# One decoder layer on one core: first heads copied within SBUF, statistics of mixer C at other hooks, output weights in rotating buffers, residual loads on the sync queue

## The chip, the core and the metric

The kernel runs on one core of one Trainium2 chip. The metric is the device time of one execution in microseconds (us); the core's five engines are TensorE (PE, with its weight loads PEld), VectorE (DVE), ScalarE (ACT), GpSimd (POOL) and SyncE (SP), and 16 DMA engines move data between DRAM and the on-chip memory SBUF. PE writes its products to PSUM, from where DVE or ACT take them. SP, ACT and POOL each have a queue of their own on which they issue DMAs, in their program's order; an instruction that waits holds up all that stand behind it on its engine.

## The reference, cut to what matters

One layer of a hybrid decoder on x (1024 positions, width 1024), all in float32:

```python
h = rmsnorm(x, norm_mix_g)
a_h, a_b, a_c, q, k, v, c_val, c_gate = split(h @ w_in)     # 256 x3, 512 x3, 256 x2
y_a = a_b * causal_dwconv(a_c * a_h, conv_a_w)              # 3 taps
y_b = dilated_mixture(q, k, v, rel_bias)                    # 8 heads of 64, three dilations
u   = causal_dwconv(c_val * sigmoid(c_gate), conv_c_w) + conv_c_b   # 31 taps
y_c = silu(layernorm(u, ln_c_g, ln_c_b))
y   = concat(rmsnorm(y_a, g_a), rmsnorm(y_b, g_b), rmsnorm(y_c, g_c))
x   = x + y @ w_out
up  = causal_dwconv(rmsnorm(x, norm_ffn_g) @ w_up, conv_f_w)
x   = x + (silu(gate) * val) @ w_down
return rmsnorm(x, final_g)
```

What matters here: y_c needs three statistics over its 256 channels one after another (the mean, the variance, then the mean square for the last norm), each of which needs the one before. q and k of a head are needed whole before its first score. And w_out is applied to y_a and y_c (128-row blocks 0, 1, 6, 7) and to y_b (blocks 2 to 5) in two separate stages.

## The kernel before, in words

Every float32 matrix product is made of three products of rounded parts: an operand is split into a high part (ACT casts it, line 71) and a low part (the difference, line 72, on POOL or DVE), and `mm3` (lines 90 to 92) adds hi x hi, hi x lo and lo x hi. A product is 128 x 128 by 128 x 512 columns.

**Input projections.** `proj` (line 252) computes one 128-column block of h @ w_in: eight steps (one for each block of 128 rows), six products in each. `load_w` brings its weights into the pair of rotating buffers `w_raw`, `w_hi`, `w_lo` (two of each), so the weights of block n+2 can be split only when the products of block n are done. After each step `proj` runs the functions that were hooked to that step. From line 421 the blocks are, with the count of their first step: `ah` of half 0 (step 8), `ac` (16), `ab` (24), `ah` of half 1 (32), `ac` (40), `ab` (48), then q and k of heads 0 and 1 (`proj_qk(0)` at 56, `proj_qk(4)` at 64), of heads 2 and 3 (`proj_qk(1)` at 72, `proj_qk(5)` at 80). The four other pairs follow during the attention (`more_qk`, line 607).

**Statistics of mixer C.** DVE does the 31 taps of the long convolution (line 298) while these blocks run, and adds the two halves (`ln_a`, line 432). `stat_hook` (line 268) hooks two things to later steps: `first`, in which PE sums over the channels (line 116, eight one-column results) and DVE and ACT finish the statistic, and then `col_to_rows`, in which PE turns the column into rows (line 137), DVE copies them, and SP writes them to DRAM and reads them back as a row for all partitions (lines 142 and 146). What follows is handed on: `ln_center` (line 447) subtracts the mean, `ln_scale` (line 453) scales and applies silu, and the last row goes to `norm` (line 435). The steps are in `HK` (line 466): `HK[0]`, `HK[1]` for the mean, counted from step 40; `HK[2]`, `HK[3]` counted from the step at which `ln_center` ran; `HK[4]`, `HK[5]` counted from the step of `ln_scale`. With 6, 8, 8, 10, 9, 11 the three sums come at steps 46, 56, 67 and the rows at 48, 58, 69. `HK[6]`, `HK[7]` (steps 61 and 65) are those of mixer A. PE's order is fixed by the program, so a statistic that isn't ready at its step stops PE.

**Heads.** `proj_qk` writes the high and low part of q and k to DRAM (`qk`, lines 397 and 398, on SP). `load_head` (line 488) brings a head's rows back as `sa` (high part of q in both halves of the partitions), `sb` (low part of q) and `sm` (high and low part of k): six transfers of 256 KB on POOL's queue, then the bias strip `g` on SP and v on POOL. It is called for heads 0 and 1 at line 516, after the last `proj_qk` and after the pools for the attention are opened.

**Attention.** PE works through chunks of scores, transposes and p x v products (lines 527, 528, 550, 581). Between them `slot` (line 713) takes steps from `fill`, that is `more_qk` and then `out_ac` (line 658): the products of y_a and y_c with w_out, in two halves of 512 output columns (`dh`), eight blocks of 128 positions (`t`) each, four products (three matmuls each) to a block. `out_ac` opens its pools in the room of the normalised input (`close(c_x)`), splits the four y tiles (two of them, of y_c, come from DRAM through `w_raw`), then loads w_out with `load_half` into `w_raw` and splits it into `wac` (dh 0) and into `w_hi`, `w_lo` (dh 1). The residual x (`xp2`, eight tiles of 512 KB) is loaded on ACT's queue, held behind the last cast of those weights (line 689), and added at line 700. `pair_den` (line 592) sends the denominators of a pair of heads to DRAM and back on SP (lines 142 and 597) and `finish_pair` (line 601) multiplies by them on DVE.

**What sets the order.** PE's order is the program's. For the other engines a planner picks at build time, from its own estimate of times, which ready instruction an engine takes next, the earlier in the program first; `issue_after` pins an instruction behind another one on its engine. So a transfer whose buffer is free is issued well ahead of its place in the program. A tile in a pool opened in the room of another pool waits only for the tiles whose room it takes.

Of the kernel before, what the change touches and what calls it, by code (L numbers as in the profile page):

```python
# [9 lines left out]
F32 = mybir.dt.float32  # L10
# [4 lines left out]
P = 128  # L15
# [21 lines left out]
def body(tc, x_t, x_n, grow, par, cst, rel, oneh, nlnc, wc, w_cols, wv, w_out, w_up, w_down, out):  # L37
# [14 lines left out]
    def close(*cms):  # L52
        for cm in cms:
            cm.__exit__(None, None, None)
# [11 lines left out]
    def f(ap):  # L66
        return ap.bitcast(F32)

    def split(src, hi, lo, lo_eng, g=None):
        if g is None:  # L70
            cp = A.copy(hi, src)  # L71
            lo_eng.tensor_tensor(out=lo, in0=src, in1=f(hi), op=ALU.subtract)  # L72
        else:
            cp = A.activation(out=hi, in_=src, func=AF.Copy, scale=g)
            V.scalar_tensor_tensor(out=lo, in0=src, scalar=g, in1=f(hi), op0=ALU.mult, op1=ALU.subtract)
        return cp
# [26 lines left out]
    def table(func, after=None):  # L103

        with tc.issue_after(mark[after].ins) if after else ExitStack():
            c = const.tile([P, 8], F32, name="st_c", tag="st_c", bufs=4)
            A.activation(out=c[:, :1], in_=ones, func=func)
# [273 lines left out]

    qk = [dr.tile([2, P, S], F32, name=f"qk{i}") for i in range(8)]

    def proj_qk(i, pos, tmp=None):
        ps = proj(pos, "qk")
        t = tmp[0] if tmp else evt("qt")
        if i < 4:
            V.scalar_tensor_tensor(out=t[:, :S], in0=ps, scalar=-0.125, in1=r1b, op0=ALU.mult, op1=ALU.mult)
        else:
            V.tensor_tensor(out=t[:, :S], in0=ps, in1=r1b, op=ALU.mult)  # L390
        if tmp:
            hi, lo = tmp[1:]
        else:
            hi = ev.tile([P, S], F32R, name="q_hi", tag="fr", bufs=6)
            lo = ev.tile([P, S], F32R, name="q_lo", tag="fr", bufs=6)
        split(t[:, :S], hi, lo, G if tmp else V)
        nc.sync.dma_start(out=qk[i][0], in_=f(hi))
        nc.sync.dma_start(out=qk[i][1], in_=f(lo))

# [61 lines left out]
    def do_norm():  # L461
        while todo:
            norm(*todo.pop())

    todo = []
    HK = (6, 8, 8, 10, 9, 11, 5, 9)
    stat_hook(lna, 1.0 / 256, None, HK[0], HK[1], ln_center)
    a_conv(1, t1)
    a_out(1, t1)
# [4 lines left out]
    do_norm()  # L474
    proj_qk(1, 9)
    do_norm()
    table(AF.Exp, "sqrt")
    proj_qk(5, 10, (yb[2], yb[3].bitcast(F32R), yb[2].bitcast(F32R)))
    close(c_ev, c_mm)
# [4 lines left out]
    for n, bufs in (("T", 2), ("S", 1), ("F", 1), ("L", 1), ("V", 2)):  # L484
        pss[n] = pool("ps" + n, space=PS, bufs=bufs)
    psS, psL, psT, psV, psF = (pss[n][1] for n in "SLTVF")

    def load_head(h):
        j, s = h // 2, (h % 2) * 64
        sa = a0.tile([P, S], F32R, name="sa", tag="sa", bufs=2)  # L490
        sb = a0.tile([P, S], F32R, name="sb", tag="sb", bufs=2)
        sm = a0.tile([P, S], F32R, name="sm", tag="sm", bufs=2)
        g = a0.tile([P, S], F32, name="g", tag="g", bufs=2)
        vv = a0.tile([P, TT, P], F32R, name="vv", tag="vv", bufs=2)
        for dst, src in ((sa, (qk[j][0], qk[j][0])), (sb, (qk[j][1], qk[j][1])), (sm, (qk[4 + j][0], qk[4 + j][1]))):
            for e in range(2):
                G.dma_start(out=dst[e * 64:(e + 1) * 64, :], in_=src[e][s:s + 64, :])
        fr = fs[h:h + 1, 1:1 + S]
        fr = bass.AP(tensor=fr.tensor, offset=fr.offset, ap=[[1, P], [1, S]])
        nc.sync.dma_start(out=g, in_=fr)  # L500
        G.dma_start(out=vv, in_=vd[:, :, h * P:(h + 1) * P].rearrange("t p c -> p t c"))
        return sa, sb, sm, g, vv

    NPT = 3
    pth = [a1.tile([P, 4 * P], F32R, name=f"pth{i}") for i in range(NPT)]
# [7 lines left out]
    den = [a1.tile([P, 16], F32, name=f"den{j}") for j in range(4)]  # L513
    mn = a1.tile([P, 64], F32, name="mn")
    SEG = {0: [256], 1: [256], 2: [384], 3: [512], 4: [512, 256], 5: [512, 256], 6: [512, 384], 7: [512, 512]}
    heads = {0: load_head(0), 1: load_head(1)}

    def score(h, qi):
        sa, sb, sm, g, _ = heads[h]
# [118 lines left out]
    def load_half(rows, dh, hi, lo):  # L638

        raw = wp.tile([P, 1024], F32, name="w_raw", tag="w_raw", bufs=2)  # L640
        nc.sync.dma_start(out=raw.rearrange("p (b c) -> p b c", b=2),
                          in_=w_out[rows * P:(rows + 2) * P, dh * 512:dh * 512 + 512]
                          .rearrange("(b p) c -> p b c", b=2))
        mark["w"] = split(raw, hi, lo, G)

    def load_row(k, hi, lo):
        raw = wp.tile([P, 1024], F32, name="w_raw", tag="w_raw", bufs=2)
# [9 lines left out]

    def out_ac():

        close(c_x)  # L660
        held["xp"], px = pool("xp", "right")
        held["wac"], pw = pool("wac", "right")
        held["yac"], pa = pool("yac", "right")
        for i in AC:
            yh[i] = pa.tile([P, S], F32R, name=f"yh{i}")
            yl[i] = pa.tile([P, S], F32R, name=f"yl{i}")
        wac = [(pw.tile([P, 1024], F32R, name=f"wac_hi{q}"), pw.tile([P, 1024], F32R, name=f"wac_lo{q}"))
               for q in range(2)]
        held["x4"] = px.tile([P, 4, S], F32, name="x4")
        xp2.extend(held["x4"][:, t, :] for t in range(4))  # L670
        for t in range(4, 8):
            xp2.append(px.tile([P, S], F32, name=f"xp{t}"))
        for i in AC:
            t = yb[2 + i] if i < 2 else wp.tile([P, 1024], F32, name="w_raw", tag="w_raw", bufs=2)
            if i >= 2:
                nc.sync.dma_start(out=t, in_=yd[i % 4])
            with tc.issue_after(mark["t"].ins), tc.issue_after(mark["v"].ins):
                split(t, yh[i], yl[i], V)
            yield 0
        for dh in range(2):  # L680
            w2 = wac if dh == 0 else [wp_pair() for _ in range(2)]
            for q, r in enumerate((0, 6)):
                load_half(r, dh, *w2[q])
            if dh:
                for q in range(2):
                    load_row(2 + q, *wac[q])
            for t in range(8):
                if dh == 0:
                    with tc.issue_after(mark["w"].ins):
                        for q in ((0, 1) if t == 0 else (t + 1,) if t < 7 else ()):  # L690
                            nc.scalar.dma_start(out=xp2[q], in_=x_n[q * P:(q + 1) * P, :])
                ps = psF.tile([P, 512], F32, name="f_ps", tag="f_ps")
                ts = slice(t * P, (t + 1) * P)
                for n, k in enumerate(AC):
                    cs = slice(n % 2 * 512, n % 2 * 512 + 512)
                    mm3(ps, yh[k][:, ts], yl[k][:, ts], w2[n // 2][0][:, cs], w2[n // 2][1][:, cs], n == 0, n == 3)
                    if n < 3:
                        yield 1
                x2 = xp2[t][:, dh * 512:dh * 512 + 512]
                V.tensor_tensor(out=x2, in0=ps, in1=x2, op=ALU.add)  # L700
                yield 2
        for q in range(2):
            load_row(4 + q, *wp_pair())

    def both():
        yield from more_qk()
# [459 lines left out]
```

## Time and profile before

| what | value |
|---|---|
| median of 3 runs | 1182.11 us (1181.99 to 1182.67) |
| the profiled execution | 1181.71 us |
| its span, first to last instruction | 1179.9 us |
| PE busy | 1138.5 us, 96% |
| DVE, ACT, POOL busy | 757.4, 503.7, 521.3 us |
| mean granted TensorE clock | 0.984 of full speed |
| DMA | 162.80 MB, mean 138 GB/s |

How to read it: a busy PE is not PE at its peak, since matmuls overlap; at full speed a 512-column matmul starts about every 0.23 us though it is shown with 0.39. [...] All times within the execution are counted from the first instruction. "DMA share" is the busy share of the 16 DMA engines, and can read above 1. In the list of waits, a line says who waited for whom, the sum, how often, and the longest.

### The profile page before, as it was taken

What the parts mean: (1) busy time and instruction counts of PE and PEld (TensorE: products, weight loads), DVE (VectorE), ACT (ScalarE), POOL (GpSimd) and SP (SyncE); (2) the same over time, 40 slices, a digit from 0 to 9 for tenths busy, and PEclk for the clock granted to TensorE, in tenths of its full rate; (3) what the DMA queues carried; (4) which work ended last, traced back from release to release, by engine and by line L of the source; (5) the groups of instructions that cost most, each with busy time, mean ns of one, the idle gap of its engine ahead of it and who ended that gap; (6) DMA issues with size and microseconds to landing.
All of it is one profiled execution on the core that took longest, in us unless ns stands there. A gap on an engine that the chain in (4) does not pass through costs nothing.

```text
span 1179.9 us, 14291 instructions
## 1 busy us (share of the span) xinstructions
PE 1138.5 (96%) x5327; PEld 943.7 (80%) x5327; DVE 757.4 (64%) x886; ACT 503.7 (43%) x798; POOL 521.3 (44%) x328
## 2 busy tenths in 40 slices
PE   9999979899979999989999999999999999999997
PEld 7888868788858887868888888888887788888886
DVE  7599965356656666796677887788778722164214
ACT  7212115256555655573444444444444432343323
POOL 4223522423222203036677777777776043334331
PEclk9999989999989999989999999999999999999999
DMA  6218214977689604223242342332423554456531
GB/s 239 86 40 234 73 53 121 309 195 166 156 236 228 143 1 161 96 102 124 78 138 89 108 141 83 133 108 90 142 89 126 169 191 158 146 188 217 171 116 72
DMA packets 59317, 162.80 MB, mean 138 GB/s; under 512 B 6232, under 2 KB 15952, under 8 KB 59248
## 3 DMA queue, kind: packets, MB, share of 16 engines
q1 hardware_dynamic: 44784, 139.27, 36.1%
q0 software_dynamic: 12160, 16.78, 7.2%
q10 hardware_dynamic: 2304, 5.83, 1.4%
q8 instruction: 42, 0.69, 0.3%
q14 instruction: 27, 0.22, 0.1%
HBM read 127.17 MB, written 34.69 MB: 137 GB/s over the span
## 4 chain that ended last, share of the span: by engine, by line
PE 83%; DVE 6%; DMA 5%; ACT 3%; issue 2%; POOL 1%; SPq 0%; ACTq 0%; DVEq 0%; POOLq 0%
PE cb L91 8%; PE cb L90 8%; PE cb L92 8%; PE d_ps L92 7%; PE d_ps L91 6%; PE d_ps L90 6%; PE ca L92 4%; PE ca L90 4%; PE ca L91 4%; PE pv_ps L581 2%; PE f_ps L90 2%; PE f_ps L92 2%; PE f_ps L91 2%; PE t_ps L550 2%; PE v L92 1%
## 5 line engine op out<-in xcount | busy, mean ns | idle before, releaser
L72 POOL TENSOR_TENSOR w_lo<-w_raw,w_hi 128x1024 fp32r<-128x1024 f32 (+2 forms) x49 | 108.7, 2220 | 204.6 <-ACT w_hi L71 204.6
L960 DVE SCALAR_TENSOR_TENSOR x<-ut,pr,x 128x1024 f32<-128x1024 f32 x88 | 147.0, 1688 | 18.8 <-ACT x L958 18.0
L72 POOL TENSOR_TENSOR wd_lo<-w_raw,wd_hi 128x1024 fp32r<-128x1024 f32 x32 | 78.4, 2454 | 163.3 <-ACT wd_hi L71 150.7
L92 PE MATMUL d_ps<-wd_hi,a_lo 128*128 128x512 f32 x336 | 131.7, 392 | 1.2 <-DVE a_lo L72 1.2
L90 PE MATMUL d_ps<-wd_hi,a_hi 128*128 128x512 f32 x336 | 131.5, 391 | 0.5 <-ACT a_hi L71 0.5
L91 PE MATMUL d_ps<-wd_lo,a_hi 128*128 128x512 f32 x336 | 131.4, 391 | 0.5 <-POOL wd_lo L72 0.5
L72 DVE TENSOR_TENSOR a_lo<-a_raw,a_hi 128x512 fp32r<-128x512 f32 x42 | 40.0, 961 | 132.4 <-ACT a_hi L71 125.3
L71 ACT CAST w_hi<-w_raw 128x512 fp32r<-128x512 f32 (+2 forms) x61 | 46.1, 764 | 138.8 <-PE v L92 23.6
L298 DVE SCALAR_TENSOR_TENSOR yc<-u,pr,yc 128x1024 f32<-128x1024 f32 x60 | 89.7, 1548 | 1.7 <-ACT yc L295 1.4
L92 PEld LDWEIGHTS d_ps<-wd_hi,a_lo 128*128 128x128 f32 x336 | 63.5, 189 | 14.6 <-DVE a_lo L72 1.5
L90 PEld LDWEIGHTS d_ps<-wd_hi,a_hi 128*128 128x128 f32 x336 | 63.5, 189 | 14.2 <-ACT a_hi L71 1.0
L91 PEld LDWEIGHTS d_ps<-wd_lo,a_hi 128*128 128x128 f32 x336 | 63.4, 189 | 13.9 <-POOL wd_lo L72 0.8
L71 ACT CAST a_hi<-a_raw 128x512 fp32r<-128x512 f32 x42 | 25.8, 620 | 111.9 <-PE d_ps L91 108.6
L958 ACT ACTIVATE x<-ut,pr 128x1024 f32<-128x1024 f32 x44 | 50.7, 1153 | 47.8 <-DVE ut L1000 32.6
L537 ACT ACTIVATE p<-p,mn 128x128 f32<-128x128 f32 (+3 forms) x64 | 49.8, 778 | 40.5 <-DVE mn L534 40.3
L1006 DVE TENSOR_TENSOR x<-x 128x1024 f32<-128x1024 f32 x22 | 46.3, 2105 | 10.6 <-ACT x L1005 10.6
L71 ACT CAST wd_hi<-w_raw 128x1024 fp32r<-128x1024 f32 x42 | 43.9, 1048 | 20.0 <-DMA w_raw<-in 20.0
L997 DVE TENSOR_TENSOR ut<-cb,yb 128x512 f32<-128x512 f32 x22 | 15.2, 690 | 56.3 <-PE cb L92 56.3
L561 DVE TENSOR_TENSOR ptl<-t_ps,pth 128x512 fp32r<-128x512 f32 x48 | 33.1, 690 | 20.6 <-ACT pth L560 20.1
L971 POOL TENSOR_TENSOR xp<-xp 128x512 f32<-128x512 f32 x11 | 21.2, 1925 | 55.2 <-DMA xp<-in 49.8
L550 PE MATMUL t_ps<-ident,p 128*128 128x128 f32 x288 | 44.4, 272 | 0.0
L534 DVE CUSTOM_DVE_ANT_0 p<-l_ps,g 128x640 f32<-128x640 f32 (+5 forms) x34 | 33.8, 995 | 15.0 <-PE l_ps L528 14.4
(405 smaller groups left out, 3319.1 us busy)
## 6 DMA issues: line engine op xcount, KB each, us to landing
w_raw<-in SPq DMA_DIRECT2D x93, 512.0 KB, 3.7
ur<-in SPq DMA_DIRECT2D x22, 512.0 KB, 3.7
xp<-in SPq DMA_DIRECT2D x22, 512.0 KB
actd<-x SPq DMA_DIRECT2D x22, 512.0 KB
a_raw<-actd SPq DMA_DIRECT2D x42, 256.0 KB, 2.8
vd<-vt SPq DMA_DIRECT2D x8, 512.0 KB
vv<-vd POOLq DMA_DIRECT2D x8, 512.0 KB, 5.4
g<-fs SPq DMA_DIRECT2D x8, 512.0 KB, 9.5
```

The source lines that it names most:

```text
L71: cp = A.copy(hi, src)
L72: lo_eng.tensor_tensor(out=lo, in0=src, in1=f(hi), op=ALU.subtract)
L90: T.matmul(ps, whi, xhi, start=start, stop=False, **kw)
L91: T.matmul(ps, whi, xlo, start=False, stop=False, **kw)
L92: T.matmul(ps, wlo, xhi, start=False, stop=stop, **kw)
L298: V.scalar_tensor_tensor(out=yc[i], in0=u[i][:, j:j + S], scalar=col("cwc", j * 2 + i), in1=yc[i], op0=ALU.mult, op1=ALU.add)
L534: V.tensor_tensor_reduce(out=p[:, :n], in0=ps[:, :n], in1=gq, op0=ALU.add, op1=ALU.min, scale=1.0, scalar=3e38, accum_out=mn[:, ix:ix + 1])
L537: mark["exp"] = A.activation(out=p[:, :n], in_=p[:, :n], func=AF.Exp, scale=-1.0, bias=mn[:, ix:ix + 1], accum_out=den[h // 2][:, dc:dc + 1])
L550: T.transpose(out=tp[:, i * P:(i + 1) * P], in_=p[:, kj * P:(kj + 1) * P], identity=ident)
L958: A.activation(out=c, in_=t[:, 2:], func=AF.Copy, scale=col("cwf", 2 * 44 + m))
L960: V.scalar_tensor_tensor(out=c, in0=t[:, q:q + S], scalar=col("cwf", q * 44 + m), in1=c, op0=ALU.mult, op1=ALU.add)
L1006: V.tensor_tensor(out=cg, in0=cg, in1=cv, op=ALU.mult)
```

## The change

Four edits. (1) The high and low parts of q and k of heads 0 and 1 stay in SBUF: `proj_qk` returns the tiles instead of writing them to DRAM, and `load_head` copies from them; the calls for heads 0 and 1 move from after the pools of the attention to before `proj_qk(5)`. (2) The hooks of mixer C become 10, 14, 7, 11, 8, 12: sums at steps 50, 61, 73, rows at 54, 65, 77. The last row now comes during `proj_qk(1)`, so its `norm` follows that block. (3) The weights of dh 0 go into the rotating `w_hi`, `w_lo`, and their loads stand first in `out_ac`, ahead of the y tiles; dh 1 uses `wac`; row blocks 2 and 3 of w_out go into the rotating buffers and row blocks 4 and 5 into `wac`; the weights are split in halves of 512 columns. (4) The residual tiles are loaded on SP's queue, no longer held behind a cast, two of them ahead of the weights of dh 1 and one more in each block `t`.

```diff
@@ load_head, moved up ahead of proj_qk; the new lines in it @@
+        q, k = qk[j], qk[4 + j]
+        for dst, src in ((sa, (q[0], q[0])), (sb, (q[1], q[1])), (sm, (k[0], k[1]))):
@@ proj_qk @@
         split(t[:, :S], hi, lo, G if tmp else V)
+        if i % 4 == 0:
+            qk[i] = hi, lo
+            return
         nc.sync.dma_start(out=qk[i][0], in_=f(hi))
@@
-    HK = (6, 8, 8, 10, 9, 11, 5, 9)
+    HK = (10, 14, 7, 11, 8, 12, 5, 9)
@@
     proj_qk(1, 9)
     do_norm()
+    heads = {0: load_head(0), 1: load_head(1)}
     table(AF.Exp, "sqrt")
     proj_qk(5, 10, (yb[2], yb[3].bitcast(F32R), yb[2].bitcast(F32R)))
@@
-    heads = {0: load_head(0), 1: load_head(1)}
@@ load_half @@
-        mark["w"] = split(raw, hi, lo, G)
+        for q in range(2):
+            q = slice(q * 512, q * 512 + 512)
+            mark["w"] = split(raw[:, q], hi[:, q], lo[:, q], G)
@@ out_ac @@
+        w2 = [wp_pair() for _ in range(2)]
+        for q, r in enumerate((0, 6)):
+            load_half(r, 0, *w2[q])
         close(c_x)
@@
         for dh in range(2):
-            w2 = wac if dh == 0 else [wp_pair() for _ in range(2)]
-            for q, r in enumerate((0, 6)):
-                load_half(r, dh, *w2[q])
-            if dh:
+            if dh == 0:
                 for q in range(2):
-                    load_row(2 + q, *wac[q])
+                    nc.sync.dma_start(out=xp2[q], in_=x_n[q * P:(q + 1) * P, :])
+                for q, r in enumerate((0, 6)):
+                    load_half(r, 1, *wac[q])
+            else:
+                w2 = wac
+                for q in range(2):
+                    load_row(2 + q, *wp_pair())
             for t in range(8):
-                if dh == 0:
-                    with tc.issue_after(mark["w"].ins):
-                        for q in ((0, 1) if t == 0 else (t + 1,) if t < 7 else ()):
-                            nc.scalar.dma_start(out=xp2[q], in_=x_n[q * P:(q + 1) * P, :])
+                if dh == 0 and t < 6:
+                    nc.sync.dma_start(out=xp2[t + 2], in_=x_n[(t + 2) * P:(t + 3) * P, :])
@@
         for q in range(2):
-            load_row(4 + q, *wp_pair())
+            load_row(4 + q, *wac[q])
```

## Rows read from the trace of the kernel before

**Rows 1.** Waits of PE: who waited for whom, us in total, times, longest.

```profile
PE st_ps L116 <- DVE ln_a L432: 7.2, 1, 7.2
PE f_ps L90 <- ACT wac_hi L71: 5.0, 1, 5.0
PE s_ps L527 <- DMA sm<-qk: 4.2, 1, 4.2
```

**Rows 2.** PE's timeline at the mean of mixer C: start, us, instruction, [idle before].

```profile
141.74 0.39 PE L90 MATMUL ac<-xh,w_hi 128*128 128x512 f32 x1
...
151.03 0.39 PE L92 MATMUL ac<-xh,w_lo 128*128 128x512 f32 x1
158.65 3.54 PE L116 MATMUL st_ps<-ones,ln_a 128*128 128x1 f32 x16 [7.23 <-DVE ln_a L432]
162.05 0.77 PE L90 MATMUL ac<-xh,w_hi 128*128 128x512 f32 x1
...
166.87 0.40 PE L92 MATMUL ab<-xh,w_lo 128*128 128x512 f32 x1
...
187.06 1.84 PE L116 MATMUL st_ps<-ones,ss_a 128*128 128x1 f32 x16
```

**Rows 3.** Timelines of POOL and DVE during and after the long convolution.

```profile
132.06 2.65 POOL L72 TENSOR_TENSOR w_lo<-w_raw,w_hi 128x1024 fp32r<-128x1024 f32 x1 [4.27 <-ACT w_hi L71]
...
132.39 4.61 DVE L298 SCALAR_TENSOR_TENSOR yc<-u,pr,yc 128x1024 f32<-128x1024 f32 x2
...
157.28 1.22 DVE L432 TENSOR_TENSOR ln_a<-yc,yc 128x1024 f32<-128x1024 f32 x1
```

**Rows 4.** Timelines of PE, ACT and DVE: rows of a statistic, then the next sum.

```profile
167.10 0.27 PE L137 MATMUL tr_ps<-ident,st_c 128*8 128x128 f32 x1
...
178.12 1.91 PE L116 MATMUL st_ps<-ones,ss_a 128*128 128x1 f32 x16
...
182.81 0.27 PE L137 MATMUL tr_ps<-ident,st_c 128*8 128x128 f32 x1
...
193.32 1.28 ACT L127 ACT_TABLE_LOAD   x1
...
195.80 1.23 DVE L378 TENSOR_TENSOR ss_a<-ss_a,ss_s 128x1024 f32<-128x1024 f32 x1 [0.75 <-ACT ss_s L377]
```

**Rows 5.** The chain of waits ahead of the attention: start, us, what.

```profile
206.18 8.95 DMA scr<-tr_r
...
216.10 7.17 DMA qk<-q_hi
...
225.01 6.32 DMA sm<-qk
```

**Rows 6.** PE's timeline at the first scores.

```profile
226.92 0.39 PE L92 MATMUL qk<-xh,w_lo 128*128 128x512 f32 x1
231.46 0.36 PE L527 MATMUL s_ps<-sm,sa 128*128 128x256 f32 x1 [4.15 <-DMA sm<-qk]
...
235.32 0.40 PE L90 MATMUL f_ps<-xh,w_hi 128*128 128x512 f32 x1
```

**Rows 7.** PE's timeline at the first products with w_out.

```profile
338.32 0.60 PE L550 MATMUL t_ps<-ident,p 128*128 128x128 f32 x4
343.95 0.80 PE L90 MATMUL f_ps<-wac_hi,yh 128*128 128x512 f32 x1 [5.02 <-ACT wac_hi L71]
...
350.80 0.57 PE L90 MATMUL f_ps<-wac_hi,yh 128*128 128x512 f32 x1
```

**Rows 8.** SP's queue at the first pair of heads: start, us of issuing, transfer.

```profile
332.24 0.85 SPq L142 DMA_DIRECT2D scr<-tr_r  x1
336.49 1.09 SPq L597 DMA_DIRECT2D rden<-scr  x2
```

**Rows 9.** Two stretches of 2 us: busy time per engine, clock, DMA share, GB/s.

```profile
326.00:328.00 2.00, 2.00 (x16) 1.87 (x15) 1.58 (x4) 1.07 (x3) 0.36 (x1) 1.00 0.95 221
...
350.00:352.00 2.00, 2.00 (x10) 1.60 (x9) 0.67 (x1) 0.58 (x1) 0.94 (x1) 0.71 1.02 405
```

More of the change, by code (lines that the diff above doesn't have):

```diff
@@ L382, in body, with load_head @@
     qk = [dr.tile([2, P, S], F32, name=f"qk{i}") for i in range(8)]
+    def load_head(h):
+        j, s = h // 2, (h % 2) * 64
+        sa = a0.tile([P, S], F32R, name="sa", tag="sa", bufs=2)
+        sb = a0.tile([P, S], F32R, name="sb", tag="sb", bufs=2)
+        sm = a0.tile([P, S], F32R, name="sm", tag="sm", bufs=2)
+        g = a0.tile([P, S], F32, name="g", tag="g", bufs=2)
+        vv = a0.tile([P, TT, P], F32R, name="vv", tag="vv", bufs=2)
+        q, k = qk[j], qk[4 + j]
+        for dst, src in ((sa, (q[0], q[0])), (sb, (q[1], q[1])), (sm, (k[0], k[1]))):
+            for e in range(2):
+                G.dma_start(out=dst[e * 64:(e + 1) * 64, :], in_=src[e][s:s + 64, :])
+        fr = fs[h:h + 1, 1:1 + S]
+        fr = bass.AP(tensor=fr.tensor, offset=fr.offset, ap=[[1, P], [1, S]])
+        nc.sync.dma_start(out=g, in_=fr)
+        G.dma_start(out=vv, in_=vd[:, :, h * P:(h + 1) * P].rearrange("t p c -> p t c"))
+        return sa, sb, sm, g, vv
     def proj_qk(i, pos, tmp=None):
@@ L486, in body @@
     psS, psL, psT, psV, psF = (pss[n][1] for n in "SLTVF")
[L488 to L502, printed above, removed]
     NPT = 3
```

## The prediction

> **What bounds the kernel now.** I read the busy shares first: PE is busy for 96% of the span, so a change pays only where PE stands still or runs slowly. The list of PE's waits then names the places: three of its waits are longer than 4 us, and each is one that this change works on, the first sum of mixer C (7.2 us), the first weights of w_out (5.0 us) and the first scores (4.2 us) [rows 1]. PE's timeline around each shows more than the wait, because PE goes on at half speed after it. A matmul of 512 columns starts every 0.227 us before the stop (41 starts from 141.74 to 151.03) and every 0.438 us behind it (11 from 162.05 to 166.87), and the sixteen one-column matmuls of a sum take 3.54 instead of 1.84 us [rows 2]. So each stop has a price of its own, the wait and the slow stretch, and I work it out from the two ends.
>
> The mean of mixer C: from 151.26 (one start after the last product) to 166.87 PE does one sum and 11 starts, 1.84 + 2.50 us of work in 15.61 us. It loses **11.3 us**, of which some 4.0 are the slow clock [rows 2].
> The first scores: from 227.15 to 235.32 it does work worth 9.5 matmuls of 512 columns, 2.16 us in 8.17. It loses **6.0 us** [rows 6].
> The first products with w_out: from 338.92 to 350.80 it does 9 of them and four half-wide ones, 2.5 us in 11.88. It loses **9.4 us** [rows 7].
> That is 26.7 us in all, the most that this change could return. Everything else PE does stays.
>
> **Part 1, the hooks.** PE reaches the first sum four steps later: 24 starts x 0.227 = 5.4 us after 151.26, at 156.7. The sum needs `ln_a`, which DVE ends at 157.28 + 1.22 = 158.50 [rows 3], and DVE has the convolution ahead of it without a gap, so it isn't earlier. The wait is 1.8 us if DVE is left alone. But the weights two blocks on are split as soon as PE is through with `ac`, and that moves from 164 to 152.6, into the end of the convolution: POOL's subtraction then runs beside the taps. At 132.06 such a subtraction took 2.65 us and two taps beside it took 4.61 [rows 3], against 1.22 for each tensor of that size alone, so it cost DVE 2.2 us and the wait would be 4.0. I take 2.9. [...] Whether the clock falls after 2.9 us no row here tells, as the three stops before were all longer; half of the 4.0 us is my term. Loss at the first sum: **4.9** (1.8 to 8.0).
>
> The second sum has seven steps behind its rows instead of eight, 42 x 0.227 = 9.5 us. Before, the rows at 167.10 led to a sum at 178.12, through the write to DRAM, the read, the centring and the squares: 11.0 us [rows 4]. PE waits **1.5** (0 to 3). Steps 61 and 65 now also hold the sums and rows of mixer A, which cost what they did.
>
> The third sum has eight steps, 10.9 us. Before, rows at 182.81 led to the finished squares at 195.80 + 1.23, 14.2 us, of which 1.3 were another statistic's table load [rows 4]: 12.9, so a wait of 2.0. The copies of the first heads now start at about that time, and a transfer beside them is slow: a 4 KB write took 8.95 us once [rows 5]. I take **3** (0 to 9, the upper end with the slow clock). The wider distance between sum and rows costs PE nothing; what lies in it is a few small DVE and ACT instructions. The last row comes two blocks before the attention and its `norm` is DVE's work of 2.5 us; DVE, in order, has the last projection's result behind it, which PE needs only 14 us later.
>
> Part 1: 11.3 - 9.4 = **1.9 us gained** (-4 to +8; the three ends don't come together).
>
> **Part 2, heads 0 and 1.** Removed: four writes of 512 KB on SP. Unchanged in number: the twelve copies on POOL, two `g` on SP, two v on POOL; only the source of the twelve is another. The chain shows why the scores were late: SP stood at the read of the last row until a 4 KB write landed (8.95 us), behind it stood k's high part (7.17 us to land), and only then could POOL fetch it (6.32 us) [rows 5]. Now the fetch waits for the split itself. Even if it began only at 216.10 and took 6.32, `sm` would be there at 222.4, ahead of 226.92 [rows 6]. POOL's copies stand between weight subtractions that are needed a block later, so they delay nothing that PE waits for. What is late next is PSUM: the last projection's result has to leave its banks, one DVE instruction of 1.2 us. I charge 0.8 of 0 to 1.3 (the upper end if the first score falls on that bank): **5.2 us gained** (4.2 to 6.0).
>
> **Part 3, w_out and the residual.** The weights of dh 0 get their loads first, and their buffers come free when `more_qk` is through, at about 329, so they are split by 334 and no longer stop PE at 338.92. The halves double the casts and subtractions of four weight tiles; they lie beside PE's work, and if that cover is gone they are in the bound below. The exchange of buffers for row blocks 2 to 5 changes no time: both pairs come free at the end of the same products.
> What is late next is the fourth y tile: its load now stands behind the second weight tile in `w_raw`, so SP issues it at about 333, close to the write of the denominators at 332.24 and their read at 336.49 [rows 8]. And the eight residual loads, free of their pin, become ready when the normalised input is done with, at 326 to 329, and go out then: 4.19 MB on SP's queue ahead of both. At 405 GB/s [rows 9] they take 10.4 us, so they end at 336.5 if nothing else moves; but at 326 the 16 engines are at 0.95 already, with 221 GB/s [rows 9], so I put the y tile's landing at 343. PE needs it two products after 338.92, at 340.8; with a cast of a microsecond it waits 3.2, and part of the slow clock follows: loss **5** (0 to 9.4, as before). ACT no longer spends time issuing these loads. Part 3: **4.4 us gained**.
>
> **Sum.** 1.9 + 5.2 + 4.4 = 11.5 us. The profiled execution took 1181.71 us (1.8 of it outside its span), so 1170.2; the median of the runs is 0.4 above it: **1170.6 us**. What a measurement of this kernel can tell from no change is about 0.2%, 2.4 us.
>
> **The rivals.**
> A. *The residual loads take back part 3 and the statistics part 1.* The y tile lands at 346 or the denominators' row holds DVE, and the three sums together lose what the one did. For it: the slow 4 KB write of rows 5 and the distances of 7 and 8 steps, each shorter than the chain it covers. Against: part 1 has 11.3 us to lose before it gives nothing. Gain 0 + 5.2 + 0.5: 1176.4. [...]
> B. *Nearly all three stops go.* POOL gives way to DVE, the latencies of the rows are a microsecond shorter, the loads land in time: gain 8 + 5.5 + 6 to 9, about 20: 1162. For it: every source of the three stops is removed by name. Against: two of the three distances in part 1 don't cover the chain in the trace.
> C. *Slower.* One mechanism, at the first y tiles: the 4.19 MB move at 221 GB/s [rows 9], 19 us, with the 2.5 MB that are moving already 11 more. The y tile lands at 358, PE stands from 340.8 to 360.3 and runs slowly for 2: 21.5 us lost for 9.4. With the other parts the kernel is 5 us slower: 1187. It decides if the y tile lands after about 353. Against: when eight such loads moved before, the rate was 405 [rows 9].
> D. *The change does not do what it says.* The planner issues the copies of the heads behind something late, since the written place isn't the issued place; the scores then still wait. 1181.7 - 1.9 - 4.4 + 0.4 = 1175.8.
>
> **How the numbers follow.** Forecast (1166 to 1174): 0.42. A: 0.25, B (under 1166): 0.16, D: 0.04, all of them faster by over 0.2%: 0.87. Same: 0.06, for A with the second and third sum at their upper ends. C, or a same that goes on to slower: 0.07. The range reaches over A and D and most of B: 1161 to 1179; below lies some 0.05, above 0.15.
>
> **What would show each step.** Right: PE's wait for `ln_a` is 2 to 4 us and small waits for `ss_a` stand at the second and third sum; no wait for `sm`; no wait for a cast of w_out at the first products, a shorter one for the fourth y tile or for a p behind it. SP's queue shows eight residual loads between 325 and 330, counted from before, and a `scr` write behind them that takes over 5 us. Wrong: the clock stays at half through several statistics (part 1 then costs), the scores wait for PSUM or for DVE at the last `norm`, or PE stops for weights of w_out as before because their buffers came free later than the end of `more_qk`.

## The result and the profile after

The change made the kernel slower: median 1188.45 us (four runs, 1187.93 to 1188.72) against 1182.05 (four runs, 1181.16 to 1182.67) of the kernel before measured beside it, a ratio of 1.0054 (95% interval 1.0037 to 1.0072). The forecast was 1170.6. The profiled execution took 1188.72 us, 1.8 of it outside its span of 1186.9 (1179.9 before).

The list of PE's waits shows the three stops of [rows 1] gone or short, and two new ones in their place (who waited for whom, us in total, times, longest):

```profile
PE st_ps L116 <- DVE ss_a L378: 13.6, 2, 13.0
PE cb L856 <- DVE b22l L72: 7.8, 1, 7.8
PE f_ps L90 <- ACT yh L71: 3.0, 1, 3.0
...
PE st_ps L116 <- DVE ln_a L452: 1.8, 1, 1.8
```

The first, the sum of squares of mixer C's third statistic, is longer than any stop that the change removed. PE's timeline through the statistics and up to the first scores (start, us, instruction, idle before it):

```profile
158.78 2.41 PE L116 MATMUL st_ps<-ones,ln_a 128*128 128x1 f32 x16 [1.82 <-DVE ln_a L452]
169.35 0.27 PE L137 MATMUL tr_ps<-ident,st_c 128*8 128x128 f32 x1
179.68 3.75 PE L116 MATMUL st_ps<-ones,ss_a 128*128 128x1 f32 x32 [0.52 <-DVE ss_a L378]
190.46 0.38 PE L137 MATMUL tr_ps<-ident,st_c 128*8 128x128 f32 x2
214.78 3.58 PE L116 MATMUL st_ps<-ones,ss_a 128*128 128x1 f32 x16 [13.05 <-DVE ss_a L378]
...
240.51 0.38 PE L531 MATMUL s_ps<-sm,sa 128*128 128x256 f32 x1 [1.32 <-DVE yb L407]
```

The first score starts at 240.51 where it started at 231.46 [rows 6]: 9.05 us lost by then, although its own wait fell from 4.15 to 1.32. What lies between the row at 190.46 and the sum at 214.78 is told by the queues of SP and POOL and by DVE:

```profile
191.19 2.18 POOL L394 DMA_DIRECT2D sa<-q_hi  x4
192.55 0.64 SPq L142 DMA_DIRECT2D scr<-tr_r  x2
198.24 0.35 SPq L146 DMA_DIRECT2D ln_r<-scr  x1
207.12 2.48 DVE L476 SCALAR_TENSOR_TENSOR yc<-yc,pr,ln_r 128x1024 f32<-128x1024 f32 x2 [14.40 <-DMA ln_r<-scr]
```

The copies of the heads and the row of the second sum left within 2 us of each other. SP could issue the row's read only 5.7 us after its write, and the row was used 8.9 us later. The write is 4 KB; the read brings 512 KB, the row for all partitions. In the kernel before the same two steps, with no copy beside them, took 1.5 and 3.8 us (SP's queue and DVE):

```profile
183.43 0.30 SPq L142 DMA_DIRECT2D scr<-tr_r  x1
184.90 0.33 SPq L146 DMA_DIRECT2D ln_r<-scr  x1
188.68 2.48 DVE L456 SCALAR_TENSOR_TENSOR yc<-yc,pr,ln_r 128x1024 f32<-128x1024 f32 x2 [5.29 <-DMA ln_r<-scr]
```

So the row cost 14.6 us where it had cost 5.3. The weights that SP loads just ahead of the row (`w_raw`, issued at 191.27) are not the cause: in the first run with the copies held back (below) they are issued as close ahead, at 189.36 for a row at 190.64, and the row takes 5.6 us. PE also ran slowly around the stop: in windows of 10 us (us, PE busy and its products, granted clock, DMA share, GB/s) the clock is 0.72 in 200 to 210 and 0.50 in 210 to 220. While the copies run the DMA engines are busy for 0.90 and 0.79 of the time and move 186 and 184 GB/s.

```profile
160.00:170.00 10.00, 10.00 (x35) 0.66 0.17 54
...
180.00:190.00 10.00, 10.00 (x53) 0.83 0.00 1
190.00:200.00 10.00, 10.00 (x47) 1.00 0.90 186
200.00:210.00 10.00, 1.74 (x8) 0.72 0.79 184
210.00:220.00 10.00, 5.22 (x20) 0.50 0.58 160
```

Right behind the first scores the lag is 7.50 us (the same transposes start at 242.66 before and at 250.16 after), as PE runs slowly there in the kernel before (clock 0.83 in 230 to 240) and no longer does (1.00 in 230 to 250). At the products with w_out it shrinks further: the sixteen transposes ahead of the feed-forward start at 497.51 in the kernel before and at 501.31 after, 3.8 later. There the second new stop adds 4.5 again, the second buffer of the next transposes (before, then after; two kernels, so two fences):

```profile
503.41 0.66 PE L846 MATMUL cb<-ident,xp 128*128 128x128 f32 x4 [1.25 <-ACT x L863]
506.96 1.12 PE L846 MATMUL cb<-ident,xp 128*128 128x128 f32 x4 [2.89 <-ACT x L863]
```

```profile
506.87 0.66 PE L856 MATMUL cb<-ident,xp 128*128 128x128 f32 x4 [0.91 <-ACT x L873]
515.31 1.08 PE L856 MATMUL cb<-ident,xp 128*128 128x128 f32 x4 [7.79 <-DVE b22l L72]
```

From these second transposes the lag is 8.35 us; 1.35 come back by the end, and 7.0 stay.

### The profile page after: what moved, and what is told of

Read it like the earlier page. It is cut to its first block, busy times and chain, and to the rows that moved or that the text cites. A ratio compares the mean times of both kernels' runs of the same rounds, so it can differ in the third digit from the quotient of the medians.

```text
span 1186.9 us, 14301 instructions
## 1 busy us (share of the span) xinstructions
PE 1139.3 (96%) x5327; PEld 944.1 (80%) x5327; DVE 754.9 (64%) x886; ACT 504.2 (42%) x802; POOL 524.0 (44%) x332
## 4 chain that ended last, share of the span: by engine, by line
PE 86%; DVE 5%; DMA 4%; ACT 3%; issue 1%; POOL 1%; SPq 0%; ACTq 0%; DVEq 0%; POOLq 0%
PE cb L90 9%; PE cb L91 9%; PE cb L92 9%; PE d_ps L92 6%; PE d_ps L91 6%; PE d_ps L90 6%; PE ca L92 4%; PE ca L90 4%; PE ca L91 4%; PE pv_ps L585 2%; PE f_ps L90 2%; PE f_ps L92 2%; PE f_ps L91 2%; PE t_ps L554 2%; DMA w_raw<-in 1%
## 5 line engine op out<-in xcount | busy, mean ns | idle before, releaser
L72 POOL TENSOR_TENSOR w_lo<-w_raw,w_hi 128x512 fp32r<-128x512 f32 (+2 forms) x51 | 108.1, 2123 | 189.9 <-ACT w_hi L71 189.9
L71 ACT CAST w_hi<-w_raw 128x512 fp32r<-128x512 f32 (+2 forms) x63 | 46.3, 747 | 132.8 <-PE v L92 23.6
```

## The experiments

My theory after the traces: the later distances put the row of the second sum beside the copies of the first heads, and this alone turns a gain into a loss; the second stop is an order of DVE's and ACT's work that the planner derives from part 3. The rival for the first: sums at these distances stop PE with or without copies. All ratios are to the kernel before measured beside the run, whose medians lay between 1182.3 and 1184.0.

**One part at a time, and the copies held back.**

```diff
# e1_hooks: the kernel before, with
+    HK = (10, 14, 7, 11, 8, 12, 5, 9)
# e2_heads: the kernel before, with proj_qk, load_head and its early call as in the change
# e3_wout: the kernel before, with load_half, wp_pair and out_ac as in the change
# e4_gate: the changed kernel, with mark["sl"] = mixer C's last Silu and, after the third do_norm()
+    gt = const.tile([P, 1], F32, name="gt")
+    with tc.issue_after(mark["sl"].ins):
+        mark["gt"] = G.tensor_copy(gt, yc[1][:, :1])
+    with tc.issue_after(mark["gt"].ins):
         heads = {0: load_head(0), 1: load_head(1)}
```

> The kernel before with the new distances of the three sums alone, (10, 14, 7, 11, 8, 12): heads and output weights as before. Theory (the row of the second sum is late because the copies of the first heads now run beside it): without those copies the row takes about what it took in the kernel before, 5.3 us from its write's issue to its first reader (183.43 to 188.68) and not the 14.6 of the changed kernel (192.55 to 207.12). The 13.05 us stop at the third sum shrinks to 2 to 4, with a slower clock for 10 us at most; the first sum gives back about 5 of its 11.3. Sum: 1181 us (1178 to 1183). Rival (the new distances are too tight by themselves): the third sum stops PE for 10 us or more here too, and the time is 1187 to 1191.

Measured: 1188.09 us, ratio 1.0038 (1.0023 to 1.0052). The third sum stopped PE for 10.52 us: the rival's number. But my premise was wrong, not the mechanism: there were copies beside the row. POOL fetched `sa` from DRAM at 190.84, as soon as q was written. The projection of q ends at the same step as ever, but ACT now casts q's high part at 186.66, ahead of mixer C's Silu, where the kernel before casts it at 196.62, behind that Silu and the squares; and the second row had moved from 183.43 to 190.42. The row took 12.8 us (POOL, SP and DVE of this run):

```profile
190.42 1.26 SPq L142 DMA_DIRECT2D scr<-tr_r  x2
190.84 2.17 POOL L497 DMA_DIRECT2D sa<-qk  x4 [2.28 <-DMA qk<-q_hi]
194.65 0.34 SPq L146 DMA_DIRECT2D ln_r<-scr  x1
...
203.22 2.48 DVE L456 SCALAR_TENSOR_TENSOR yc<-yc,pr,ln_r 128x1024 f32<-128x1024 f32 x2 [13.19 <-DMA ln_r<-scr]
```

So the hooks alone make a loss, and copying within SBUF is not needed for it. They do not make all of it. By the medians this run loses 4.9 us and the next two, with the other parts alone, gain 3.5 and 0.5: 0.9 lost in all, 5.5 less than the 6.4 of the whole change. The stop at the third sum is 13.05 in the whole and 10.52 here (in an execution of 1183.99 us, 4.1 under the run's median); the rest of the 5.5 us stays open.

> The kernel before with the early head copies out of SBUF alone; old distances of the sums, old output weights. Theory: by the old distances the row of the second sum has landed at 188.7, before the q halves exist (about 197.7), so the copies meet only rows that PE doesn't wait for; the 6.0 us loss at the first scores goes but for about 1: 1177 us (1175 to 1180). Rival (copies within SBUF are dear wherever they stand): the scores or a sum wait as long as before, 1182 or more.

Measured: 1179.69 us, ratio 0.9969 (0.9955 to 0.9984), a gain of 3.5 us against the kernel before, where 5 were expected. No wait stands at the first scores any more, but the first score starts at 231.68, no earlier than before: the row of the third sum waits 3.67 us for DVE, which now takes the normalization of mixer A ahead of the statistic and stands there until mixer A's row has come. That row takes 5.0 us from its read's issue (197.65 to 202.69) where it took 4.8 (198.46 to 203.26), so it is DVE's order and not a slower row. What is gained is the faster clock behind (230 to 240: 1.00 where it was 0.83).

> The kernel before with the change of the output product alone (weights for the first half in the rotating pair, second half in the other, residual loads on SP). Theory: the stops at the first output products lose 5 of their 9.4 us, and the stop of 7.8 us in the transposes ahead of the feed-forward product (L856 of the changed kernel) appears here too, against 4.1 in the kernel before, since the order of DVE's and ACT's work there follows from this part: 1181.5 us (1179 to 1184). Rival (that stop comes from the shift of everything ahead of it): it stays at 4.1, and the time is 1177.

Measured: 1182.62 us, ratio 0.9996 (0.9982 to 1.0010). The stop for `b22l` is there with the same 7.79 us, with hooks and heads as before, so it comes from this part and eats what the part gains: the theory, with its size.

> The changed kernel with one GpSimd copy of one column of the normalized mixer C (which exists after the late row has been used) ahead of the copies of the first heads, so that they start after it. Theory: the row takes 5 to 6 us again in place of 14.6, the 13.05 us stop at the third sum falls to 2 to 4, the scores don't wait for the copies by more than 2: about 9 us off, 1179.5 us (1177 to 1183). Rival (the row is late for another reason, the distances or what else the queues carry): the stop stays over 9 us and the time at 1187 or more.

Measured: 1191.76 us, ratio 1.0075 (1.0051 to 1.0098). The row behaved as the theory says: written at 190.64, used at 196.26, 5.6 us, and the stop was 3.59 us. But the holding copy read mixer C after its last normalization, so the head copies started only at 224.26, and the scores waited 9.54 us for them (PE and POOL):

```profile
203.93 3.58 PE L116 MATMUL st_ps<-ones,ss_a 128*128 128x1 f32 x16 [3.59 <-DVE ss_a L378]
...
224.26 1.22 POOL L394 DMA_DIRECT2D sa<-q_hi  x2
...
237.89 0.55 PE L535 MATMUL s_ps<-sm,sa 128*128 128x256 f32 x1 [9.54 <-DMA sm<-q_lo]
```

**The hold earlier, the order mended, and both.** The mended order:

```diff
# in feature_major
             A.copy(q1, bk[0])
+            put("b22", bk[1])
             put("t2", t2)
             V.tensor_tensor(out=q1, in0=bk[1], in1=q1, op=ALU.subtract)
-            put("b22", bk[1])
# in lead_weights
+        with tc.issue_after(mark["norm"].ins) if j == 2 else ExitStack():
             return operand(raw[:, HS[0]], V if j < LEAD else G), operand(raw[:, HS[1]], G if j % 2 and j >= LEAD else V)
```

> As the run with the copies held back, but the GpSimd copy that holds them reads mixer C right after its Silu, not after its last normalization; there the holding copy came at 224, and the sixth projection's scores waited 9.5 us for the halves. Theory: the copies start at 202 to 212, the row of the second sum takes 5 to 6 us, the stop at the third sum stays near 3.6 (13.05 in the changed kernel), and the scores wait under 2: 9 to 10 us under the changed kernel, 1179 us (1176 to 1182) where the kernel before has 1182. Rival (held copies only move the wait to the scores): the scores wait over 6 us and the time stays at 1185 or more.

Measured: 1189.79 us, ratio 1.0046 (1.0033 to 1.0060). The stop at the third sum was 4.64 us, the row 6.6 us. But now the third row fell beside the copies, which with v's loads filled the DMA engines from 200.69 to about 216 (DMA share 0.98 in 200 to 210 and 1.31 in 210 to 220): its write left at 214.63, its read could be issued at 223.82, and DVE used it at 228.56; behind that stood the last projection's result, for which the scores waited 6.40 us. Moving the copies moved the meeting to the next row. That is the rival's wait; the total also holds something else (below).

> The run with the output product's change alone, and in feature_major the split of the second quadrant moved ahead of two others and the casts of the third lead weight ordered behind the last normalization, so that the buffer that the next transposes wait for comes free earlier. Theory (the 7.8 us stop is an order of DVE and ACT and nothing else): the stop falls to 2 to 4, the time is 4 to 6 us under that run, 1177 us (1174 to 1180). Rival (the stop is set by data that are late, the operand tiles in reused space): it stays over 6 us and the time within 1.5 of that run.

Measured: 1181.89 us, ratio 0.9986 (0.9972 to 1.0001). The stop fell to 3.85 us as expected, an order it is; but only 1.2 of the 4 us lie in the medians, which the two intervals can't tell from nothing: 26 us later PE waits 2.46 us for `t2l`, whose split is now behind.

> The changed kernel with the old distances of the sums and the order in feature_major mended as in the other run. Theory (the parts add up where the second row stays clear of the copies): heads alone gave 3.5 us, the output product with the mended order should give 5: 1173.5 us (1170 to 1177). Rival (the parts share their gain, since what is saved ahead of attention is waited for at the output product): 1177 or more.

Measured: 1176.99 us, ratio 0.9941 (0.9917 to 0.9965), 7.0 us under the kernel before: the version is faster than both kernels. The median lies on the border of the two forecasts; that the single gains, 3.5 for the heads and 2.1 for the output product with the mended order, come to 5.6 speaks for adding up.

> The changed kernel with the copies held back until after Silu and the order in feature_major mended, both together. Theory: 9 us and 5 us off the changed kernel, 1174 us (1171 to 1178). Against the run with the old distances it tells what the new distances are worth when no copy runs beside the second row: first sum 1.8 in place of 7.2 and its slow clock, against a stop of 3.6 at the third: within 3 us of it either way.

Measured: 1187.40 us, ratio 1.0032 (1.0019 to 1.0045): 13 us from the forecast. The third stop was 5.03, the scores waited 6.57, as in the run before with a hold; the mended order took 2.4 us off it.

**The row out of the way, the copies where they are.** With 14, 7, 9, 9, 11 the second row comes at step 63 in place of 65, the third sum at 72 in place of 73 and the third row at 74 in place of 77.

```diff
# e9_rows: the changed kernel; e10_rows_fm: with the mended order too; e11_before_rows: the kernel before
+    HK = (10, 14, 7, 9, 9, 11, 5, 9)
```

> The changed kernel with two of its distances altered: the rows of the second sum 9 steps after the start in place of 11, the third sum 9 after the row in place of 8, (10, 14, 7, 9, 9, 11). Theory (what counts is whether the second row lands before the copies of the first heads start, at about 191): its write is issued at 184 to 186 in place of 192.55, it is read 5 to 6 us later, and the 13.05 us stop at the third sum falls to under 2; the gain at the first sum (1.8 in place of 7.2 and a shorter time at the lower clock) stays. 1175.5 us (1172 to 1180), the upper end for a third row that is late beside the copies. Rival (sums this late stop PE at any spacing): the third stop stays over 6 us, 1183 or more.

Measured: 1179.31 us, ratio 0.9960 (0.9938 to 0.9982), where the changed kernel has 1.0054. Two steps of the second row, one of the third sum and three of the third row are together worth 11 us. The row took 5.8 us and the stop was 0.68 (SP, DVE, PE, POOL):

```profile
188.12 0.29 SPq L142 DMA_DIRECT2D scr<-tr_r  x1
190.19 0.32 SPq L146 DMA_DIRECT2D ln_r<-scr  x1
...
193.96 2.48 DVE L476 SCALAR_TENSOR_TENSOR yc<-yc,pr,ln_r 128x1024 f32<-128x1024 f32 x2 [3.03 <-DMA ln_r<-scr]
...
200.76 2.18 POOL L394 DMA_DIRECT2D sa<-q_hi  x4 [9.73 <-ACT q_hi L71]
200.84 1.95 PE L116 MATMUL st_ps<-ones,ss_a 128*128 128x1 f32 x16 [0.68 <-DVE ss_a L378]
```

My number for the write's issue (184 to 186) was off by 2 to 4 us; the lower clock behind the double sum (0.83 in 180 to 190) is part of that. The copies themselves moved too, from 191 to 200.76, since ACT takes the cast of q's high part behind the Silu and the squares of the third sum (at 199.43, in the changed kernel at 189.17). So this run clears the row of the copies from both sides; the two holds are the runs that move the copies alone.

> The same with the order in feature_major mended. Theory: 1 to 4 us under the run without it (the stop of 7.8 falls to 3.9, and in the run with the output product alone 1.2 of it reached the end): 1173 us (1169 to 1177), and so under the run with the old distances and the mended order, by the gain at the first sum. Rival (what is saved at the first sum is waited for at the scores or the output product): equal to that run, a ratio of about 0.994 to the kernel before.

Measured: 1177.44 us, ratio 0.9946 (0.9928 to 0.9964). That it lies under the run with the old distances did not come true: 0.9946 and 0.9941 can't be told apart.

> The kernel before with (10, 14, 7, 9, 9, 11) and nothing else; where (10, 14, 7, 11, 8, 12) alone made it 0.4% slower. Theory: the second row lands before the loads of the first heads start (190.8 in that run), the third sum stops PE for under 2 us in place of 10.5, and the first sum's gain shows: 4 to 5 us under the kernel before, ratio 0.996 (0.994 to 0.999). Rival (later sums are a loss by themselves): ratio 1.000 or more.

Measured: 1181.21 us, ratio 0.9989 (0.9971 to 1.0008). The third sum's stop is 0.98 us, but the gain at the first sum hardly reaches the end; the row of the third sum waits 4.89 us.

> The run with altered distances and mended order, with mixer A's sum two steps later, (.., 7, 9) for its (.., 5, 9), so that it no longer stands right behind mixer C's second sum; its row stays where it was. In that run and in the changed kernel the two sums stand back to back (32 products of one column, 3.75 to 5.4 us), and the clock of 180 to 190 was 0.66 to 0.83 where the kernel before, with the sums apart, has 1.00. Theory (the gain at the first sum is given back there): the clock of 180 to 190 is 1.00 again, 2 to 3.5 us less: ratio 0.992 (0.990 to 0.9945). Rival (the gain goes elsewhere, to the third row's wait of 3.4 and the scores): ratio within 0.0015 of 0.9946.

The edit: `HK[6]`, `HK[7]` from 5, 9 to 7, 9. Measured: 1174.83 us, ratio 0.9941 (0.9922 to 0.9961), the best median of all, within 0.0005 of the run without it. The clock of 180 to 190 was 0.83, not 1.00. So the rival holds. Nor do two sums have to stand back to back for the clock to fall: here it read 0.65 and 0.50 in 180 to 182 and 182 to 184, behind one sum (177.79) and ahead of mixer A's (184.10).

Where the gain goes can be followed against the run with the old distances and the mended order (PE at the second transposes and at `t2l`; this run, then that one):

```profile
495.00 1.09 PE L856 MATMUL cb<-ident,xp 128*128 128x128 f32 x4 [3.85 <-DVE x L876]
521.15 0.50 PE L91 MATMUL cb<-t2l,w_hi 128*128 128x512 f32 x1 [2.46 <-DVE t2l L72]
```

```profile
503.11 1.09 PE L856 MATMUL cb<-ident,xp 128*128 128x128 f32 x4 [3.85 <-DVE x L876]
```

This run is 8.1 us ahead at the second transposes (1.8 of it from before the first sum) and 2.5 at the end (spans of 1172.5 and 1175.0). Of the 5.6 us between, 2.46 are the wait for `t2l`, which the other run does not have, and the clock reads 0.69 in 520 to 525 and 0.66 in 935 to 940 where the other has 1.00, some 1.7 us each. The run with altered distances and mended order has the same wait at 526.17: it is 3.0 us ahead at the second transposes (1.1 of it from before the first sum) and 0.5 behind at the end. So there is a gain ahead of attention, and it is lost in the feed-forward stage, not at the row of the third sum, which waits 5.37 us here but 3.33 in the run with the old distances too.

**The price of the hold itself.** What was open, and the two runs:

```diff
# e13_gate_wide: the run with the earlier hold, with
-        gt = const.tile([P, 1], F32, name="gt")
+        gt = const.tile([P, 16], F32, name="gt")
# e14_col: the changed kernel, with
+    gt = const.tile([P, 1], F32, name="gt")
+    G.memset(gt, 0.0)
```

> The run with the copies held back until after Silu, with the tile that the holding copy writes 16 columns wide in place of 1 (one column of it written), so that all tiles behind it lie 64 bytes further and not 4. Theory A (the one-column tile shifts the operands of the products and these then come 0.233 us apart in place of 0.227): the products of 590 to 650 are 266 again, the time falls by 5 to 7 us to 1183.5 (1181 to 1185.5), about the kernel before; what is left of the loss is the wait of 6.4 at the scores. Theory B (these products are slower because of the later copies or by chance): 262 to 263 products, 1189 or more.

Measured: 1188.66 us, ratio 1.0055 (1.0032 to 1.0078), 263 products between 590 and 650. Widening the tile did not bring the pace back.

> The changed kernel with a one-column tile allocated and cleared once, and nothing else. Theory A: 262 to 263 products between 590 and 650 in place of 266, all stops ahead of attention as in the changed kernel, 5 to 7 us over it: 1194.5 us (1192.5 to 1196.5). Theory B: 266 products and 1188.5.

Measured: 1190.80 us, ratio 1.0078 (1.0056 to 1.0101), 263 products; its stops are the changed kernel's (12.63 us at the third sum, 7.79 at the transposes). A window of this run, then of the changed kernel:

```profile
590.00:650.00 60.00, 60.00 (x263) 1.00 0.35 112
```

```profile
590.00:650.00 60.00, 60.00 (x266) 1.00 0.33 105
```

With one unused column in SBUF the products between 530 and 930 start 0.2303 us apart on average in place of 0.2267 (some of them 0.235; the 0.233 of the forecast is too much), at the same clock; from 960 on they start 0.2267 apart in both kernels. Over some 1750 products that is 6 us: from the second transposes to the end the run takes 677.4 us (511.52 to 1188.9), the changed kernel 671.6. By the medians the difference of the two kernels (2.4 us) is within their intervals, as this execution was 2.8 us quicker between the first score and the transposes. The three other runs with a one-column tile have the same 0.2303, and no run without a tile has it. So 5 to 6 us of the runs with a hold are this tile and not the hold: in the earlier hold the first score, at 234.31, is 6.2 us ahead of the changed kernel's, and the second transposes, at 510.50, are 4.8 ahead, which is lost again by the end. Why the tile costs this, no run tells; with 16 columns in place of one the pace is 0.2298.

## Why the prediction was wrong

By its own steps, with the slow clock in each term as there (a window at 0.66 counts 3.4 us, at 0.83 1.7):

- **First sum: right.** Wait 1.82, the lower end. POOL's subtraction did not run beside the taps: it started at 162.16, behind POOL's product for mixer A at 159.85, which waits for DVE, so the upper end did not come into play. Earlier in this trace each of the two engines is once the slower one: two taps beside the subtraction of 132.16 (2.69 us) took 4.61 us together, as in [rows 3]; at 138.59 a product of POOL took 8.16 us (2.39 at 167.36) beside five taps of 1.21 each. What decides which of them is slowed, no run shows. Slow clock 3.4 in 160 to 170, more than the half of 4.0 that I charged, and partly chance: after the same wait of 1.82 the run with the hooks alone kept 1.00 there. 5.2 lost where I had 4.9.
- **Second sum: right.** Wait 0.52 and 1.7 of clock, 2.2 for 1.5 (0 to 3).
- **Third sum: the step that failed.** "I take 3 (0 to 9, the upper end with the slow clock)": it cost 13.05 and 3.3 of slow clock, 16.4. The sentence ahead of it named the cause, that the copies start then and a write beside them is slow, with 8.95 us for one in [rows 5]. I put the slowness on the write alone and discounted it to 1 us over the 2.0 without copies. Both halves of the row are slow beside copies, the write by 4.2 us and the read by 5.1. That they would meet follows from the steps for the row (65) and the end of q's projection (64); what the prediction does not look at is ACT's order, which casts q at 189.17, ahead of the late Silu, where the kernel before casts it behind that Silu at 196.62.
- **First scores: right.** 1.32 us for a PSUM bank where I charged 0.8 of 0 to 1.3.
- **Sum of these.** 11.3 + 6.0 of losses gone, 5.2 + 2.2 + 16.4 + 1.3 = 25.1 new: 7.8 us slower. The first score is 9.05 us late, and 1.85 of the 6.0 lay behind that point, so 9.6 by this account; 7.8 is what should be left behind the scores, where 7.50 is measured.
- **w_out and residual: right in size, the way there partly luck.** I put the fourth y tile's landing at 343; it was 351.2 on a clock 7.5 later, 343.7. The wait is 3.04 where I had 3.2. The lag falls from 7.50 to 3.8: 3.7 gained for 4.4 (the 1.5 before that are the slow clock behind the first scores, part 2). But the eight residual loads did not all go ahead of the y tile: three were issued from 332.33 to 333.25 and one at 339.28, the other four behind it, and the tile itself took 11.3 us to land (SP and ACT, changed kernel):

```profile
339.84 0.33 SPq L685 DMA_DIRECT2D w_raw<-yd  x1
...
351.21 1.04 ACT L71 CAST yh<-w_raw 128x1024 fp32r<-128x1024 f32 x1 [3.82 <-DMA w_raw<-yd]
```

Rival C's mechanism, a landing after 353, did not happen, though its 1187 is near the measured number.
- **"The exchange of buffers changes no time": the second failure.** Part 3 leads the planner to order DVE and ACT otherwise 150 us later; which of its edits does so, the exchange, the halves or the loads on SP, no run takes apart. In feature_major ACT casts the high part of `b22` only at 510.78, and then DVE has the split `t4l` of an operand tile and the last normalization (line 844, 2.28 us beside POOL, 1.29 in the kernel before) ahead of the `b22` split, which frees the buffer that PE waits for:

```profile
510.78 0.58 ACT L71 CAST b22h<-cb 128x512 fp32r<-128x512 f32 x1
510.91 1.45 DVE L72 TENSOR_TENSOR t4l<-x,t4h 128x512 fp32r<-128x512 f32 x1 [0.23 <-ACT t4h L71]
512.28 2.28 DVE L844 SCALAR_TENSOR_TENSOR xp<-xp,rcol,g2row 128x1024 f32<-128x1024 f32 x1
514.48 0.68 DVE L72 TENSOR_TENSOR b22l<-cb,b22h 128x512 fp32r<-128x512 f32 x1
```

The run with the output product alone has this stop with its 7.79 us, and the one with the mended order has it halved, so that it comes from part 3 and is a matter of order is shown. No term of the sum and no rival held such an effect outside the stages that the diff names.

Rival A said that statistics take back part 1, and gave it no more than that; it lacked that they can take more than there was to gain. Shown are: the row's 14.6 us beside copies and 5.3 to 6.7 without (the holds, the altered distances), the stop that follows, and the 11 us between 1.0054 and 0.9960. The gain at the first sum (some 6 us by the changed kernel's own trace) does not reach the end in the runs with altered distances and mended order; it is lost behind the second transposes, at the wait for `t2l` and the lower clock. Not settled are why the planner's order leaves that wait there and not in the run with the old distances, and the 5.5 us by which the whole change is slower than its three parts.

## What to carry to other kernels

Before a statistic that goes through DRAM is moved, lay the time of its write and read beside every large copy that becomes ready in the same 15 us, and charge both halves of the trip at the slow price (here 14.6 us beside copies, 5.3 without); here it was cheaper to move the row ahead of the copies than to hold the copies, which then met the next row. Look also at what the moved work stood in front of: with the statistic later, ACT cast q earlier, and the copies started 10 us sooner. A gain in one stage is safe only when the stages behind it do not give it back. And a change of buffers can reorder a planner's work far behind it: look for PE's waits that are new in stages that the diff does not touch.

## What the runs showed of the hardware that was not expected

- A 4 KB write and the 512 KB read behind it, on SP's queue, took 5.7 and 8.9 us beside copies of POOL's queue (changed kernel), 1.5 and 3.8 without them (kernel before). The third row's write took 8.95 us in the kernel before [rows 5]; until its read was issued 9.2 passed in the earlier hold, 9.7 with the altered distances and 10.5 with the wider tile. Why a small write takes so long beside copies is not shown: no run here takes the copies' writes apart from the rest.
- The twelve copies of heads 0 and 1 occupied the DMA engines longer within SBUF than from DRAM, for the same bytes and the same distances of the sums. In the list of queues for 185 to 245 us (packets, MB, share of 16 engines), the changed kernel and then the run with the hooks alone:

```profile
q0 software_dynamic: 960, 3.15, 26.2%
```

```profile
q0 software_dynamic: 960, 3.15, 23.6%
```

With the old distances it is 23.6% (heads alone) against 21.2% (the kernel before), with the altered ones 28.5% against 24.9%.

- Two statistics summed back to back (32 products of one column, 3.75 to 5.4 us in all) came with a clock of 0.66 to 0.83 in the window of 180 to 190, in the changed kernel and all nine others that have them so; in the kernel before and the four other runs with the old distances, where the sums are 9 us apart, it stayed at 1.00. With the two sums 6 us apart it was still 0.83, and fell behind one sum alone, so that standing back to back lowers the clock is not shown.
- With one column more in SBUF the feed-forward products of 530 to 930 us started 0.2303 us apart in place of 0.2267, some 6 us over the stage.
